# Softmax over rows of 1024: larger tiles, looped groups of four rows, and sixteen partitions of the first load sent ahead

## Chip, cores, metric

One core of a Trainium2 chip. The metric is device time in microseconds of one execution; executions of one kernel agree within 0.35% here. A packet below is one contiguous piece that one of the sixteen DMA engines moves; a wave is sixteen packets, one on each engine.

## The reference

```python
x = np.random.randn(32, 512, 1024).astype(np.float32)      # temperature 0.5
scaled = x / temperature
shifted = scaled - np.max(scaled, axis=-1, keepdims=True)
exp_x = np.exp(shifted)
return exp_x / np.sum(exp_x, axis=-1, keepdims=True)
```

16,384 rows of 4 KB are read once and written once, 134.22 MB in all. Laid over 128 partitions that is 128 rows per partition.

## The kernel before

A ring of six slots in SBUF, eight rows per partition in each. SyncE issues the loads, GpSimd the stores, VectorE takes the maxima and scales, ScalarE takes the exponentials with their sums.

```python
SLOTS, ROWS = 6, 8
GROUPS = [4, 2, 2]
# ... cut: sizes, tiles, semaphores
def dram(t, i):
    return t[P*ROWS*i : P*ROWS*(i+1), :].rearrange("(p k) d -> p k d", p=P, k=ROWS)

for i in range(tiles):                       # SyncE: loads
    if i >= SLOTS:
        nc.sync.wait_ge(stored[i % SLOTS], 16 * (i // SLOTS))
    nc.sync.dma_start(out=slot(i), in_=dram(xf, i)).then_inc(loaded[i % SLOTS], 16)
# ... cut: TensorE passes the loads on to VectorE in order
nc.gpsimd.wait_ge(loaded[2], 16)             # GpSimd: stores, from the third load on
for i in range(tiles - 1):
    nc.gpsimd.wait_ge(scaled, len(groups) * (i + 1))
    nc.gpsimd.dma_start(out=dram(of, i), in_=slot(i)).then_inc(stored[i % SLOTS], 16)

with nc.vector.Fori(0, tiles) as t:          # VectorE: groups written out
    take(nc.vector, ready)
    for a, k in groups:                      # maximum, then bias = -scale * maximum
        ...
    for a, k in groups:                      # wait for the sums, reciprocal, scale the rows
        ...
# ... cut: ScalarE, one activation per row; the last tile is stored by SyncE
```

Of the kernel before, what the change touches and what calls it, by code (L numbers as in the profile page):

```python
# [1 line left out]

# [4 lines left out]



SLOTS, ROWS = 6, 8  # L10

GROUPS = [4, 2, 2]


@with_exitstack
def kernel(
    ctx: ExitStack,
    tc: tile.TileContext,
    x: bass.AP,
    temperature: bass.AP,  # L20
    out: bass.AP,
):
    nc = tc.nc
    f32 = mybir.dt.float32
    scale = 1.0 / float(temperature)
    extreme = mybir.AluOpType.max if scale > 0 else mybir.AluOpType.min

    P = 128
    xf = x.flatten_outer_dims()
    of = out.flatten_outer_dims()  # L30
    n, d = xf.shape
    tiles = n // (P * ROWS)
    assert tiles * P * ROWS == n and sum(GROUPS) == ROWS
    groups = [(sum(GROUPS[:g]), k) for g, k in enumerate(GROUPS)]
    of_group = dict(groups)

    pool = ctx.enter_context(tc.tile_pool(name="data", bufs=1))
    ring = pool.tile([P, SLOTS * ROWS, d], f32, name="ring")
    top = pool.tile([P, ROWS], f32, name="top")
    bias = pool.tile([P, ROWS], f32, name="bias")  # L40
    sums = pool.tile([P, ROWS], f32, name="sums")
    recip = pool.tile([P, ROWS], f32, name="recip")
    warm = pool.tile([P, 1], f32, name="warm")



    loaded = [tc.alloc_semaphore(f"loaded{s}") for s in range(SLOTS)]
    stored = [tc.alloc_semaphore(f"stored{s}") for s in range(SLOTS)]
    ready, topped, biased, summed, inverted, scaled, finished = (
        tc.alloc_semaphore(name)  # L50
        for name in ("ready", "topped", "biased", "summed", "inverted", "scaled", "finished")
    )

    def dram(t, i):
        return t[P * ROWS * i : P * ROWS * (i + 1), :].rearrange("(p k) d -> p k d", p=P, k=ROWS)

    def slot(i):
        s = i % SLOTS
        return ring[:, ROWS * s : ROWS * (s + 1), :]

    def take(engine, sem, count=1):

        engine.wait_ge(sem, count).then_inc(sem, -count)  # L63

    with tc.tile_critical(no_gpsimd_drain=True):  # L65

        for i in range(tiles):
            if i >= SLOTS:
                nc.sync.wait_ge(stored[i % SLOTS], 16 * (i // SLOTS))
            nc.sync.dma_start(out=slot(i), in_=dram(xf, i)).then_inc(loaded[i % SLOTS], 16)  # L70
        for i in range(tiles):
            nc.tensor.wait_ge(loaded[i % SLOTS], 16 * (i // SLOTS + 1)).then_inc(ready, 1)


        nc.gpsimd.wait_ge(loaded[2], 16)
        for i in range(tiles - 1):
            nc.gpsimd.wait_ge(scaled, len(groups) * (i + 1))
            nc.gpsimd.dma_start(out=dram(of, i), in_=slot(i)).then_inc(stored[i % SLOTS], 16)  # L78

        with nc.vector.Fori(0, tiles) as t:  # L80
            first = t % SLOTS * ROWS
            take(nc.vector, ready)
            for a, k in groups:
                nc.vector.tensor_reduce(  # L84
                    out=top[:, a : a + k],
                    in_=ring[:, bass.ds(first + a, k), :],
                    axis=mybir.AxisListType.X,
                    op=extreme,
                ).then_inc(topped, 1)
                take(nc.vector, topped)  # L90
                nc.vector.tensor_scalar_mul(  # L91
                    bias[:, a : a + k], in0=top[:, a : a + k], scalar1=-scale
                ).then_inc(biased, k)
            for a, k in groups:
                take(nc.vector, summed, k)
                nc.vector.reciprocal(  # L96
                    recip[:, a : a + k], sums[:, a : a + k]
                ).then_inc(inverted, 1)
                take(nc.vector, inverted)
                for b in range(a, a + k):  # L100
                    row = ring[:, bass.ds(first + b, 1), :]
                    ins = nc.vector.tensor_scalar_mul(row, in0=row, scalar1=recip[:, b : b + 1])  # L102
                ins.then_inc(scaled, 1)


        nc.scalar.activation(  # L106
            warm, nc.const_aps.tensor(0.0, (P, 1)), mybir.ActivationFunctionType.Exp
        )
        with nc.scalar.Fori(0, tiles) as t:
            first = t % SLOTS * ROWS  # L110
            for b in range(ROWS):
                row = ring[:, bass.ds(first + b, 1), :]
                if b in of_group:
                    take(nc.scalar, biased, of_group[b])
                nc.scalar.activation(  # L115
                    row,
                    row,
                    mybir.ActivationFunctionType.Exp,
                    bias=bias[:, b : b + 1],
                    scale=scale,  # L120
                    accum_out=sums[:, b : b + 1],
                ).then_inc(summed, 1)


        i = tiles - 1
        nc.sync.wait_ge(scaled, len(groups) * tiles)
        nc.sync.dma_start(out=dram(of, i), in_=slot(i)).then_inc(finished, 16)
        for i in range(tiles - SLOTS, tiles - 1):
            nc.sync.wait_ge(stored[i % SLOTS], 16 * (i // SLOTS + 1))
    with tc.tile_critical(no_gpsimd_drain=True):  # L130
        nc.sync.wait_ge(finished, 16, synchronizes=[nc.sync.lower_ap(slot(tiles - 1))])


# [1 line left out]
_INS = ['x', 'temperature']  # L135
_OUTS = [((32, 512, 1024), 'float32')]

_NUMBERS = {'temperature': 0.5}


# [26 lines left out]
```

## Time and profile before

| what | value |
|---|---|
| median time, span of the profiled run | 318.5 us, 316.4 us |
| data moved, plateau rate | 134.22 MB, 434 GB/s |
| VectorE, ScalarE busy | 77%, 47% |
| data packets per DMA engine | 256 of 32 KB, 1.213 us each |
| first data packet starts, last one ends | 1.96 us, 314.6 us |

The kernel is a stream through sixteen DMA engines that are occupied from the second microsecond until 314.6 us.

### The profile page before, as it was taken

How to read it: one execution, taken by the hardware profiler on the slowest of the kernel's cores; microseconds unless marked ns; L12 is line 12 of the kernel's file. 1: busy time of each engine (PE TensorE's matmuls, PEld its weight loads, DVE VectorE, ACT ScalarE, POOL GpSimd, SP SyncE). 2: the span in 40 equal slices, each digit the busy share in tenths (PEclk: the TensorE clock that was granted, in tenths of full speed). 3: DMA queues.
4: the chain of work that ended last, by engine and by line, in shares of the span. 5: the costliest groups of instructions: out<-in, count | busy, mean ns of one | idle time of the engine just before them, and what ended most of it. 6: DMA issues, size and time to landing. Idle time of an engine off the chain costs nothing. (4 is left out here: it accounts for less than half of the span.)

```text
span 316.4 us, 1208 instructions
## 1 busy us (share of the span) xinstructions
DVE 244.4 (77%) x272; ACT 148.1 (47%) x258; POOL 8.3 (3%) x19
## 2 busy tenths in 40 slices
DVE  0299999999999999996959959598695977959600
ACT  1065555556464747380834709156090651907400
POOL 0000000000000000000000000000000000000000
DMA  8999999999999999999999999999999999999995
GB/s 319 410 456 406 398 447 414 456 406 456 423 447 418 439 435 431 439 423 443 418 443 418 452 414 456 423 439 427 435 443 418 447 418 443 418 452 406 456 423 253
DMA packets 4608, 134.22 MB, mean 424 GB/s; under 512 B 512, under 2 KB 512, under 8 KB 512
## 3 DMA queue, kind: packets, MB, share of 16 engines
q1 hardware_dynamic: 2448, 71.30, 52.7%
q0 software_dynamic: 2160, 62.92, 46.1%
HBM read 67.11 MB, written 67.11 MB: 424 GB/s over the span
## 5 line engine op out<-in xcount | busy, mean ns | idle before, releaser
L115 ACT ACTIVATE ring<-ring,bias x128 | 145.1, 1135 | 147.1 <-ACTq L63 147.1
L84 DVE TENSOR_REDUCE top<-ring 128x2 f32 (+1 forms) x48 | 143.8, 2996 | 39.4 <-DVEq L63 39.4
L102 DVE TENSOR_SCALAR ring<-ring,recip x128 | 89.1, 749 | 7.2 <-DVEq L63 1.8
L115 ACT ACTIVATION_READ_ACCUMULATOR ring<-ring,bias 128x1 f32 x128 | 24.0, 187 | 0.0
L78 POOL DMA_DIRECT2D out_dram<-ring x15 | 8.1, 542 | 271.1 <-DVE ring L102 238.5
L91 DVE TENSOR_SCALAR bias<-top 128x2 f32<-128x2 f32 (+1 forms) x48 | 8.2, 170 | 7.2
L96 DVE RECIPROCAL recip<-sums 128x2 f32<-128x2 f32 (+1 forms) x48 | 7.9, 164 | 0.0
L106 ACT ACT_TABLE_LOAD x1 | 1.3, 1283 | 0.9 <-SPq L65 0.9
L106 ACT ACTIVATE warm<-const-float32-0.0 128x1 f32<-128x1 f32 x1 | 0.2, 203 | 0.0
L148 POOL MEMSET const-float32-0.0<- 128x1 f32 x1 | 0.1, 99 | 0.2 <-issue 0.2
L148 POOL MEMSET const-bfloat16-1.0<- 128x1 bf16 x1 | 0.1, 102 | 0.0
L148 POOL MEMSET const-float32-1.0<- 128x1 f32 x1 | 0.1, 99 | 0.0
L148 POOL MEMSET const-uint8-127<- 128x1 uint8 x1 | 0.1, 99 | 0.0
## 6 DMA issues: line engine op xcount, KB each, us to landing
ring<-in_x_dram SPq DMA_DIRECT2D x16, 4096.0 KB, 49.4
out_dram<-ring POOLq DMA_DIRECT2D x15, 4096.0 KB, 44.0
out_dram<-ring SPq DMA_DIRECT2D x1, 4096.0 KB, 16.8
```

The source lines that it names most:

```text
L78: nc.gpsimd.dma_start(out=dram(of, i), in_=slot(i)).then_inc(stored[i % SLOTS], 16)
L84: nc.vector.tensor_reduce(out=top[:, a : a + k], in_=ring[:, bass.ds(first + a, k), :], axis=mybir.AxisListType.X, op=extreme,).then_inc(t ...
L91: nc.vector.tensor_scalar_mul(bias[:, a : a + k], in0=top[:, a : a + k], scalar1=-scale).then_inc(biased, k)
L96: nc.vector.reciprocal(recip[:, a : a + k], sums[:, a : a + k]).then_inc(inverted, 1)
L102: ins = nc.vector.tensor_scalar_mul(row, in0=row, scalar1=recip[:, b : b + 1])
L106: nc.scalar.activation(warm, nc.const_aps.tensor(0.0, (P, 1)), mybir.ActivationFunctionType.Exp)
L115: nc.scalar.activation(row, row, mybir.ActivationFunctionType.Exp, bias=bias[:, b : b + 1], scale=scale, accum_out=sums[:, b : b + 1],).th ...
L148: nc = _bacc.Bacc("TRN2", target_bir_lowering=False, num_devices=1)
```

## The change

The intent: fewer and larger transfers (tiles of twelve rows in four slots, the same ring bytes), shorter code (loops over groups in place of groups written out), and an earlier start: sixteen partitions, one for each DMA engine, are sent ahead of the rest of the first load.

```diff
-SLOTS, ROWS = 6, 8
-GROUPS = [4, 2, 2]
+TILES = [12] * 10 + [8]
+SLOTS = 4
+GROUP = 4
+AHEAD = 16
...
+            if i == 0:
+                nc.sync.dma_start(
+                    out=slot(0)[:AHEAD], in_=dram(xf, 0)[:AHEAD]
+                ).then_inc(opened, 16)
+                nc.sync.dma_start(
+                    out=slot(0)[AHEAD:], in_=dram(xf, 0)[AHEAD:]
+                ).then_inc(loaded[0], 16)
+            else:
+                nc.sync.dma_start(out=slot(i), in_=dram(xf, i)).then_inc(loaded[i % SLOTS], 16)
+        nc.tensor.wait_ge(opened, 16)
...
-            for a, k in groups:
+            with loop_groups(nc.vector, t) as g:
+                group = bass.ds(g * GROUP, GROUP)
                 # maximum and bias of one group, at register offsets
...
-            for a, k in groups:
+            with loop_groups(nc.vector, t) as g:
                 # reciprocal and scaling of one group
...                                        (ScalarE: the same loop, one semaphore count per group)
```

## The prediction

> **What bounds the kernel now.** I read the page first, then its DMA part, the windows, the GpSimd timeline and the packet records of the trace.

> ```profile
> span 316.4 us, 1208 instructions
> DVE 244.4 (77%) x272; ACT 148.1 (47%) x258; POOL 8.3 (3%) x19
> ...
> DMA  8999999999999999999999999999999999999995
> GB/s 319 410 456 406 398 447 414 456 406 456 423 447 418 439 435 431 439 423 443 418 443 418 452 414 456 423 439 427 435 443 418 447 418 443 418 452 406 456 423 253
> DMA packets 4608, 134.22 MB, mean 424 GB/s; under 512 B 512, under 2 KB 512, under 8 KB 512
> ...
> out_dram<-ring SPq DMA_DIRECT2D x1, 4096.0 KB, 16.8
> ```

> The reader is to see that the row of DMA digits is full from the second slice to the last but one, while no compute engine passes 77%. The kernel reads 67.11 MB and writes as much, and that is all its time is. Of the 4608 packets, 512 are the 4-byte semaphore writes of 32 transfers (16 each) and 4096 carry data, 256 per DMA engine, each 32 KB: one partition's eight rows.

> ```profile
> 0.00:5.00 5.00, 0.00 (x0) 1.49 (x2) 0.20 (x4) 1.00 0.62 210
> 5.00:10.00 5.00, 0.00 (x0) 0.00 (x0) 0.00 (x0) 1.00 1.05 452
> ...
> 100.00:200.00 100.00, 84.86 (x99) 54.27 (x96) 2.67 (x5) 1.00 1.00 434
> 200.00:280.00 80.00, 62.61 (x70) 36.65 (x64) 2.67 (x5) 1.00 1.00 434
> ...
> 310.00:317.00 7.00, 0.00 (x0) 0.00 (x0) 0.00 (x0) 1.00 0.40 173
> ```

> The last two numbers of each line are the DMA share and GB/s. The rate is 434 in the long middle, where loads and stores share the engines (short stretches jump about, as whole packets are counted in them). So 434 is this kernel's plateau, and 134.22 MB at 434 is 309.3 us. What is above it, 316.4 - 309.3 = 7.1 us, is all that any change to the schedule can win (2.2%). The packet records split it: the first data packet starts at 1.96 us, the sixteen engines begin within 0.8 us of each other, and their first packets take 1.4 to 2.5 us where later ones take 1.213 (about 0.7 us per engine lost). When the first store begins, around 35 to 38 us, some 29 packets are stretched, 0.9 us per engine. The engines end between 313.2 and 314.6, and the last completion is seen at 315.06 (298.21 + 16.8). Then 1.3 us to the end. The run is 1.8 us longer than the span (318.14 against 316.4); I carry that.

> ```profile
> 46.35 0.53 POOL L78 DMA_DIRECT2D out_dram<-ring  x1 [12.62 <-DVE ring L102]
> 62.45 0.53 POOL L78 DMA_DIRECT2D out_dram<-ring  x1 [15.57 <-DVE ring L102]
> ...
> 240.37 0.53 POOL L78 DMA_DIRECT2D out_dram<-ring  x1 [18.82 <-DVE ring L102]
> 259.74 0.53 POOL L78 DMA_DIRECT2D out_dram<-ring  x1 [18.84 <-DVE ring L102]
> 279.10 0.53 POOL L78 DMA_DIRECT2D out_dram<-ring  x1 [18.83 <-DVE ring L102]
> ```

> Two regimes: early stores come every 16.1 us, the pace of VectorE on a full ring; late ones every 19.36 us, the time of 8.39 MB at 433 GB/s, sixteen packets of 1.21 us on each engine. Two transfers' semaphore writes are inside that period and add nothing visible. GpSimd's idle time is put down to VectorE, but the pace is the DMA's.

> [...]

> **The change part by part.** Ring bytes are unchanged (48 rows per partition). One row of all partitions is 0.524 MB, 1.209 us at the plateau.

> 1. Larger packets. Ten tiles of 48 KB packets and one of 32 KB: per engine 2 x (10 x 8 + 8) = 176 packets, not 256. [...]
> 2. Fewer transfers: 22 + 1 (the split load) against 32, nine semaphore writes fewer on each engine at 9 ns: 0.1 us.
> 3. Sixteen partitions ahead. The first issue takes 0.38 us and packets begin 0.63 us after it, four of the engines 0.6 us after the others. With one descriptor per engine I estimate 0.2 to 0.4 us earlier: 0.3 us. The next issue follows after some 0.4 us and its descriptors are there before the first 48 KB packet (1.81 us) is done.
> 4. VectorE. A four-row group costs 4.70 us start to start for maximum and bias (13.71 to 18.41 us), a two-row group 2.58; reciprocal and scaling 2.98 and 1.64. Their sum for eight rows is 16.12, the early pace. Groups of four alone: 7.68 per four rows, 23.0 for twelve, 1.92 us per row against 2.015. [...] The DMA needs 24 x 1.209 = 29.0 us for the load and store of such a tile. [...] ScalarE needs 12 x 1.135 = 13.6 us, and its sums are ready before VectorE ends the maxima.
> 5. Does the coarser ring starve the DMA? By hand, both queues sharing equally when both have work: the third load lands at 2.7 + 36 x 1.21 + 0.6 = 46.8 us, the first store moves data from about 51 (before, too, its first packet at 37.3 came 4.2 us after its issue at 33.05). [...] The store queue starts stores 0 to 3 at 51, 75, 101 and 130 us: always after they are computed. The load queue is briefly empty around 71 to 78 us, between the fourth load and the first free slot, but stores flow then. Later loads are back to back, 29.0 us each. The last load (eight rows) is in at 273; VectorE is free at 278, and the last eight rows are done 17 to 19 us later, at 295 to 297. By then stores 8 and 9 would last until 302.6. So 5 us of queued stores cover the last tile's compute; before, the same cover was also 5 us (the last store issued at 298.2, the older stores alone would have lasted to 303.6). No gap.

> Sum: 0.4 + 0.1 + 0.3 = 0.8 us less, 317.8 us.

> **The rivals.** (a) [...] Against it: nothing in the trace; only that a start trimmed this finely would hardly have been left with so plain a loss[...]. I give it three in ten.
> (b) VectorE becomes the pace: if a loop turn costs 1 us[...], a tile takes 29 us, the cover of stores at the end is gone, and the last store starts 3 to 6 us late: 321 to 324 us. Against it: VectorE is 77% busy, and scalings of four rows (2.74 us) can hide the next turn's bookkeeping. One in twenty.
> (c) The start is worth more: the stretched first packets and the stretch at the first store come later or smaller, and the engines end closer together. All of it is 0.7 + 0.9 + about 1 us; winning half would give 316.5 us. One in six.

> **Range and chances.** The most that can be won is 2.2% and the parts I can size win 0.25%, so faster by over 2% is 2%. Slower by over 2% means more than 6.4 us lost, which only the harder half of (a) gives, with a little of (b): 14%. The rest, 84%, is within 2%. I put the point at 318.0, a little above the sum for the sake of (a), and the range at 316.3 to 324.5, skewed upwards for the same reason.

> **What would show it.** Right: 2816 data packets (3184 with the semaphore writes), a first slice a little above 319 GB/s, 434 in the middle, stores every 29.0 us, and the last store landing within a microsecond of 315 less 0.8. Wrong by (a): a first slice far below 319 GB/s, the first sixteen packets taking several times 1.8 us, engines ending microseconds apart. Wrong by (b): VectorE over 90% busy, DMA digits under 9 in the last fifth, and the last store issued after the previous one has landed.

The sum is 0.8 us less: 0.4 us for larger packets, 0.1 us for fewer semaphore writes (a 4-byte write takes 9 ns in the trace before) and 0.3 us for the earlier start, an estimate from the issue and start times beside it. The times of VectorE in step 5, from 278 us on, are an estimate that contains the cost of the loop turns. Rival (a) is that the sixteen partitions, and the 112 after them, load at a lower rate than all 128 together.

## The result

333.22 us median (332.77 to 333.88, six runs) against 318.48 us (318.01 to 318.76, six runs): ratio 1.0465, 95% interval 1.0451 to 1.0479. It is slower by 14.7 us and outside the predicted range.

From the page of the changed kernel:

```profile
span 331.4 us, 1879 instructions
DVE 237.5 (72%) x224; ACT 149.9 (45%) x258; POOL 5.7 (2%) x14
...
DMA  9898999999999999999999999999999999999996
GB/s 142 208 273 225 421 427 457 403 463 398 463 421 433 427 427 445 409 451 415 451 403 463 427 427 445 421 445 409 457 433 421 451 437 401 445 451 398 463 378 265
DMA packets 3184, 134.22 MB, mean 405 GB/s; under 512 B 368, under 2 KB 368, under 8 KB 368
```

The reader is to see the first four slices (0 to 33 us). The DMA digits say 9, 8, 9, 8: the engines are occupied. The GB/s below them say 142, 208, 273, 225, a third to two thirds of the plateau. From the fifth slice on the kernel runs as before. The packets number 3184, as predicted; what changed is how long the first ones took. The windows of the changed kernel (last two columns: DMA share, GB/s):

```profile
0.00:10.00 10.00, 0.00 (x0) 1.49 (x2) 0.20 (x4) 1.00 1.04 157
10.00:20.00 10.00, 0.00 (x0) 0.00 (x0) 0.00 (x0) 1.00 0.88 231
20.00:30.00 10.00, 0.00 (x0) 0.00 (x0) 0.00 (x0) 1.00 1.02 241
...
100.00:200.00 100.00, 85.02 (x83) 51.62 (x91) 2.13 (x4) 1.00 1.00 431
```

In the first 30 us, 6.3 MB arrive. At 434 GB/s from 2 us on it would have been 12.2 MB, and the missing 5.9 MB are 13.6 us of the plateau. The packet records agree. A 48 KB packet takes 1.815 us in the middle; the first sixteen, which began between 1.98 and 2.94 us, took 6.06 us on average, the next seven waves (the other 112 partitions) 2.6 to 4.35 us, the first wave of the second load 2.5 us, and from there on 1.82. Summed, the packets that began in the first 35 us took 15.6 us per engine more than their size calls for, against 0.7 us in the kernel before. Of the 15.6 us, 4.2 lie on the sixteen partitions sent ahead, 10.7 on the 112 behind them and 0.7 on the next wave: most of the loss is on the larger part. After 35 us it is 1.2 us here and 0.8 us before. The first packet did not begin earlier either: 1.98 us, where it was 1.96.

### The profile page after: what moved, and what is told of

It is laid out like the page before. It is cut to its first block, busy times and chain, and to the rows that moved or that the text cites. A ratio compares the mean times of both kernels' runs of the same rounds, so it can differ in the third digit from the quotient of the medians.

```text
span 331.4 us, 1879 instructions
## 1 busy us (share of the span) xinstructions
DVE 237.5 (72%) x224; ACT 149.9 (45%) x258; POOL 5.7 (2%) x14
## 2 busy tenths in 40 slices
DMA packets 3184, 134.22 MB, mean 405 GB/s; under 512 B 368, under 2 KB 368, under 8 KB 368
## 3 DMA queue, kind: packets, MB, share of 16 engines
HBM read 67.11 MB, written 67.11 MB: 405 GB/s over the span
## 5 line engine op out<-in xcount | busy, mean ns | idle before, releaser
L109 DVE TENSOR_REDUCE top<-ring x32 | 141.4, 4417 | 50.2 <-DVEq L70 34.9
L126 DVE TENSOR_SCALAR ring<-ring,recip x128 | 87.7, 749 | 13.2 <-DVEq L70 13.2
L142 ACT ACTIVATION_READ_ACCUMULATOR ring<-ring,bias x128 | 23.9, 187 | 0.0
L122 DVE RECIPROCAL recip<-sums x32 | 5.5, 173 | 8.0 <-DVEq L70 8.0
L116 DVE TENSOR_SCALAR bias<-top x32 | 5.5, 170 | 7.4 <-DVEq L70 7.4
L102 POOL DMA_DIRECT2D out_dram<-ring x10 | 5.5, 546 | 292.3 <-DVE ring L126 229.2
## 6 DMA issues: line engine op xcount, KB each, us to landing
ring<-in_x_dram SPq DMA_DIRECT2D x1, 4096.0 KB, 30.6
out_dram<-ring SPq DMA_DIRECT2D x1, 4096.0 KB, 13.7
```

The costliest lines, as they stand in the source:

```text
L109: nc.vector.tensor_reduce(out=top[:, group], in_=ring[:, bass.ds(first + g * GROUP, GROUP), :], axis=mybir.AxisListType.X, op=extreme,).th ...
L116: nc.vector.tensor_scalar_mul(bias[:, group], in0=top[:, group], scalar1=-scale).then_inc(biased, 1)
L122: nc.vector.reciprocal(recip[:, group], sums[:, group]).then_inc(inverted, 1)
L126: ins = nc.vector.tensor_scalar_mul(row, in0=row, scalar1=recip[:, bass.ds(g * GROUP + b, 1)])
L142: ins = nc.scalar.activation(row, row, mybir.ActivationFunctionType.Exp, bias=bias[:, column], scale=scale, accum_out=sums[:, column],)
```

## The experiments

My theory at this point was rival (a) of the prediction: the partitions that a load spans set its rate, and both the sixteen ahead and the 112 after them load at a lower rate than all 128. In the expectations below, its name and the mechanism that I gave for it, which no run shows, are cut; what follows a mark in the texts of e1 to e6 is what this theory expects. Its factors of two (e4, e6) and four (e5) were assumptions then; the measured ones stand below each text. Rival 1: the twelve-row tiles or the loops cost the time. Rival 2: any small, odd or additional first transfer costs it.

### e1_no_ahead: the split undone alone

```diff
-                (the two transfers of the first load)
+                nc.sync.dma_start(out=slot(0), in_=dram(xf, 0)).then_inc(loaded[0], 16)
-        nc.tensor.wait_ge(opened, 16)
```

> The changed kernel with the first load in one piece again. [...] the first packets take under 2.5 us, 434 GB/s from the second slice on, and the time is 317.8 us, between 317 and 319, against 333.2 for the changed kernel. Rival 1 (twelve-row tiles in four slots, or the looped groups, cost the time): it stays near 330 or above.

Measured: 319.45 us (five runs), ratio to before 1.0031 (1.0017 to 1.0045). The changed kernel's ratio is 1.0465, so the split alone costs 0.0434 x 318.5 = 13.8 us. Rival 1 is out as the main cause. The time stays 1.6 us above the 317.8 that I expected, just outside my 317 to 319; the runs e8 and e9 are about that.

```profile
0.00:10.00 10.00, 0.00 (x0) 1.49 (x2) 0.20 (x4) 1.00 0.85 329
10.00:20.00 10.00, 0.66 (x1) 0.00 (x0) 0.00 (x0) 1.00 1.04 452
20.00:30.00 10.00, 8.52 (x4) 4.64 (x8) 0.00 (x0) 1.00 0.98 423
```

The same windows as above: the DMA share is much the same, the rate 1.8 to 2.1 times as high.

### e2_before_ahead: the split alone, on the kernel before

```diff
+            if i == 0:
+                nc.sync.dma_start(out=slot(0)[:16], in_=dram(xf, 0)[:16]).then_inc(opened, 16)
+                nc.sync.dma_start(out=slot(0)[16:], in_=dram(xf, 0)[16:]).then_inc(loaded[0], 16)
... (cut: the other loads as they were; TensorE waits for `opened`)
```

> The kernel before with nothing but its first load split at partition 16, so packets of 32 KB. [...] the loss is proportional to the bytes of the first tile, eight rows in place of twelve, two thirds of the 15 us: 318.5 + 10 = 328.5 us, first packets near 4 us each where they took 1.9. Rival 1: 318.5, no change. Rival 2 (a fixed cost of a short or odd-sized transfer, not of its bytes): 318.5 + 15 = 333.

Measured: 326.68 us, ratio 1.0257, which is 8.2 us more. The first sixteen packets took 3.66 us on average. With two thirds of the bytes in the tile, the cost is 0.59 of 13.8 us: nearer to the 10 us of a cost that goes with the bytes than to the 15 us of a fixed cost of a transfer. It also shows the cost without the larger tiles and the loops.

### e3_ahead_rows: two transfers, each over all partitions

```diff
-                    out=slot(0)[:AHEAD], in_=dram(xf, 0)[:AHEAD]
+                    out=slot(0)[:, :GROUP], in_=dram(xf, 0)[:, :GROUP]
-                    out=slot(0)[AHEAD:], in_=dram(xf, 0)[AHEAD:]
+                    out=slot(0)[:, GROUP:], in_=dram(xf, 0)[:, GROUP:]
```

> The changed kernel with the first load split by rows: four rows of all 128 partitions go ahead, then eight rows. Two transfers as in the change, but each spans all partitions. [...] as without a split, 317.8 us, within 0.5 of the run without a split. Rival 2 (any small or second first transfer costs): above 325.

Measured: 319.36 us, ratio 1.0025, the same as without a split (1.0031). A second, smaller transfer in front costs nothing when it spans all the partitions. It gains nothing either: the first packet begins at 1.95 us. Its first window:

```profile
0.00:10.00 10.00, 0.00 (x0) 1.49 (x2) 0.20 (x4) 1.00 0.84 324
```

### e4_ahead_64: two equal halves

```diff
-AHEAD = 16
+AHEAD = 64
```

> The changed kernel with 64 partitions ahead in place of 16, so both parts are equal, even powers of two. [...] each packet takes 2 x 1.815 = 3.6 us and the twelve rows take 29 us in place of 14.5: 317.8 + 14.5 = 332.3 us. Rival 2 in its form 'the odd 112 or the tiny 16 are slow': near 318, as no part is odd or tiny.

Measured: 333.73 us, ratio 1.048, which is 14.3 us above the run without the split (14.5 expected). The eight first waves took 3.55 to 3.84 us per packet, 2.0 to 2.1 times 1.815; the next took 2.3 us, and from there on it was 1.82. No part is odd or tiny here, so with e3 rival 2 is out.

### e5_blocks and e6_strided: the same eight parts, in two places

Both load the first tile in eight transfers of sixteen partitions; the packets and the bytes are the same.

```diff
+                for part in range(8):                     # e5_blocks: neighbours
+                    nc.sync.dma_start(out=slot(0)[16*part : 16*part + 16], in_=(the same rows)) ...
+                for part in range(8):                     # e6_strided: every eighth partition
+                    nc.sync.dma_start(out=slot(0)[part:128:8], in_=(the same rows)) ...
... (cut: the two transfers that go; TensorE waits for all eight parts)
```

> The changed kernel with its first load in eight parts of sixteen neighbouring partitions. [...] all twelve rows at a quarter of the rate, 58 us in place of 14.5: 319.4 + 43.5 = 363 us, packets of 7.2 us. A theory of a cost per extra transfer (about 14 us for the first extra one): 319.4 + 7 x 14 = 417 us, or 333 if it is paid once.

> The same eight parts of sixteen partitions and the same packets, but each part takes every eighth partition[...]. [...] half the rate, 29 us in place of 14.5: 319.4 + 14.5 = 334 us, packets of 3.6 us. If the number of parts, of partitions in a part or the issue of them mattered and not their places: the same as the eight blocks of neighbours.

Measured: 359.01 us (ratio 1.1274) and 334.05 us (ratio 1.0495). The windows of e5_blocks, then of e6_strided:

```profile
10.00:20.00 10.00, 0.00 (x0) 0.00 (x0) 0.00 (x0) 1.00 0.69 79
20.00:30.00 10.00, 0.00 (x0) 0.00 (x0) 0.00 (x0) 1.00 1.39 157
30.00:40.00 10.00, 0.00 (x0) 0.00 (x0) 0.00 (x0) 1.00 0.69 79
```

```profile
0.00:10.00 10.00, 0.00 (x0) 1.49 (x2) 0.20 (x4) 1.00 0.92 192
10.00:20.00 10.00, 0.00 (x0) 0.00 (x0) 0.00 (x0) 1.00 0.96 202
20.00:30.00 10.00, 0.00 (x0) 0.00 (x0) 0.00 (x0) 1.00 1.15 236
```

A window counts a packet whole, so with packets of 6.9 us it swings between 79 and 157. The packet records give the rates. Sixteen packets, 0.786 MB, take 6.9 us on sixteen neighbours (114 GB/s), 3.82 us on every eighth partition (206 GB/s) and 1.815 us over all 128 (433 GB/s). That is close to a quarter, a half and the whole (0.26, 0.48 and 1). The number of parts and of partitions in them is equal in both kernels, so it is the places that count. The cost of e5_blocks over the run without a split is 39.6 us and not 43.5, mostly because sixteen packets moved at 114 GB/s and not at the quarter of 434, 108.5, that I had expected.

### e10_swap: SBUF partitions or HBM addresses?

e5 and e6 differ in the HBM addresses that a part reads as well. Here a part writes sixteen neighbours in SBUF and reads every eighth stretch of HBM; the first tile's rows come out permuted. Against e5_blocks:

```diff
-                        out=slot(0)[16*part : 16*part + 16], in_=dram(xf, 0)[16*part : 16*part + 16]
+                        out=slot(0)[16*part : 16*part + 16], in_=dram(xf, 0)[part:128:8]
```

> The eight parts of sixteen neighbouring partitions again, but each part reads every eighth of the 128 stretches of HBM that the strided parts read (the first tile's rows come out in another order, a wrong result on purpose). If the partitions of SBUF decide the rate: as the eight blocks, 359 us, packets of 6.9 us. If the addresses in HBM decide it: as the strided parts, 334 us, packets of 3.8 us.

Measured: 358.28 us (ratio 1.1249), packets of 6.85 us; the result is wrong. The SBUF side decides. One of its windows, as in e5_blocks:

```profile
10.00:20.00 10.00, 0.00 (x0) 0.00 (x0) 0.00 (x0) 1.00 0.69 79
```

### e7_mid: the split in the middle of the stream

```diff
+MID = 6
-            if i == 0:
+            if i == MID:          # the split of the load, and its wait, at the seventh tile
```

> The changed kernel with the split (16 and 112 partitions) moved from the first load to the seventh, in the middle, where stores flow on the other queue. If a slow packet holds its engine back and nothing fills the time: the same 13.8 us as at the start, 333 us. [...] half of it, 324 to 328 us. If stores hide it: 319.4 us.

Measured: 328.58 us, ratio 1.0315, which is 9.0 us above the run without the split. A third less is lost than at the start. The second case of the expectation, half of it, was for stores that take up part of the time; its wording is cut. That the stores on the other queue use this third is my reading; no run shows it apart. Between 140 and 150 us the rate still fell to 216 GB/s, so the estimate of half was a little too hopeful.

```profile
140.00:150.00 10.00, 7.94 (x16) 4.84 (x10) 0.00 (x0) 1.00 0.74 216
```

### e8_loops_only: loops, with tiles of eight rows

```diff
-TILES = [12] * 10 + [8]
-SLOTS = 4
+TILES = [8] * 16
+SLOTS = 6                       # on e1_no_ahead
```

> No split, tiles of eight rows in six slots as before, but the looped groups of four rows. The run without the split was 0.3% slower than the kernel before. If the tile size is what costs that (the last store starts later and meets stretched packets, coarser packets end further apart): 318.5 us, ratio 1.000. If the loops cost it: 319.4, ratio 1.003.

Measured: 327.70 us, ratio 1.0293 (1.0279 to 1.0307). Neither expectation held. The windows of the end:

```profile
300.00:305.00 5.00, 4.59 (x2) 4.63 (x8) 0.00 (x0) 1.00 1.07 459
305.00:310.00 5.00, 2.92 (x5) 4.63 (x8) 0.00 (x0) 1.00 0.00 0
310.00:315.00 5.00, 2.92 (x5) 0.00 (x0) 0.00 (x0) 1.00 0.24 105
315.00:320.00 5.00, 0.00 (x0) 0.00 (x0) 0.00 (x0) 1.00 0.98 419
```

The DMA engines stand still for some eight microseconds while VectorE and ScalarE finish the last tile: all earlier stores have landed by 306.5 us, and the last is issued at 313.59.

```profile
313.59 0.35 SPq L149 DMA_DIRECT2D out_dram<-ring  x1
```

The timeline of VectorE for one tile of this kernel (start, length, what, idle time before):

```profile
201.16 4.41 DVE L103 TENSOR_REDUCE top<-ring  x1
205.80 0.17 DVE L110 TENSOR_SCALAR bias<-top  x1 [0.24 <-DVEq L70]
206.49 4.42 DVE L103 TENSOR_REDUCE top<-ring  x1 [0.52 <-issue]
211.14 0.17 DVE L110 TENSOR_SCALAR bias<-top  x1 [0.23 <-DVEq L70]
211.71 0.18 DVE L116 RECIPROCAL recip<-sums  x1 [0.40 <-DVEq L70]
212.30 2.74 DVE L120 TENSOR_SCALAR ring<-ring,recip  x4 [0.41 <-DVEq L70]
216.63 0.18 DVE L116 RECIPROCAL recip<-sums  x1 [1.59 <-DVEq L70]
217.22 2.74 DVE L120 TENSOR_SCALAR ring<-ring,recip  x4 [0.41 <-DVEq L70]
219.87 4.41 DVE L103 TENSOR_REDUCE top<-ring  x1
```

A tile takes 219.87 - 201.16 = 18.71 us where the written-out groups took 16.12. The short idle times in brackets, 0.2 to 0.5 us, come with the loops; in the kernel before, VectorE waits at most 0.2 us within a tile. The 1.59 us before the second reciprocal is another thing: it cannot start until ScalarE has summed the group whose bias it got at 211.3. That wait has a second cause that I overlooked: the edit also changes the groups of a tile from 4, 2, 2 to 4, 4, so the last group has twice the rows to sum. No run has groups 4, 4 written out. An estimate from the traces: in e9_unrolled the second bias ends 9.4 us into a tile, four rows take ScalarE 4.5 us, the reciprocal and scaling of a group 3.0 us, and two hand-overs some 0.3 us each, together 17.5 us. Then about half of the 2.6 us would be the grouping and half the loops. 18.71 us is still under the 19.36 us that the DMA needs for a tile, and I had stopped at that comparison. But VectorE starts at 14.0 us, after the first load, and 14.0 + 16 x 18.71 = 313.4 us is when it ends. At the estimated 17.5 us it would be 294 us, so by this estimate the store is late only with the loops. Being faster than the DMA per tile is not enough; the gain over all the tiles must also cover the first load and the last store.

### e9_unrolled: twelve-row tiles, groups written out

```diff
-            with loop_groups(nc.vector, t) as g:        # on e1_no_ahead; ScalarE likewise
+            for a, k in [(0, 4), (4, 4), (8, 4)]:       # the last tile: (0, 4), (4, 2), (6, 2)
```

> No split, the twelve-row tiles in four slots, but the groups written out as before (4, 4, 4; the last tile 4, 2, 2). VectorE should take 23.0 us a tile (7.68 per four rows) where the loops take 26.2, and the last store be issued near 297 us in place of 302.4. If the loops are what made the run without the split 0.3% slower than before: 317.8 us, ratio 0.998. If the coarser tiles are: 319.4, ratio 1.003. Could be the fastest of all.

Measured: 318.39 us, ratio 0.9995 (0.9981 to 1.0009); the early stores come every 23.05 us and the last is issued at 297.01. Together with e8 this gives a square, as ratios to before:

| | groups written out | looped groups of four |
|---|---|---|
| tiles of eight rows | 1 (the kernel before, groups 4, 2, 2) | 1.0293 (groups 4, 4) |
| tiles of twelve rows | 0.9995 (4, 4, 4; last tile 4, 2, 2) | 1.0031 (4, 4, 4; last tile 4, 4) |

The larger tile alone changes nothing that can be measured. The looped groups cost 2.9% on eight-row tiles, there together with the coarser grouping, and 0.4% on twelve-row tiles, where only the last tile is grouped otherwise. The timeline of VectorE in e1_no_ahead shows why the twelve rows soften it:

```profile
193.31 0.18 DVE L116 RECIPROCAL recip<-sums  x1 [0.60 <-DVEq L70]
193.90 2.74 DVE L120 TENSOR_SCALAR ring<-ring,recip  x4 [0.41 <-DVEq L70]
196.56 0.17 DVE L116 RECIPROCAL recip<-sums  x1
197.14 2.74 DVE L120 TENSOR_SCALAR ring<-ring,recip  x4 [0.41 <-DVEq L70]
```

With a third group there is time for the sums: no 1.59 us before the second reciprocal. A tile takes 26.23 us, 2.19 us per row against 2.34 with eight rows. VectorE then ends early enough: the last store is issued at 302.43 us, and the older stores land only at 307.7. What the remaining 0.4% of e1_no_ahead is made of is not settled. Its trace has 0.55 us per engine of stretched packets where the last store begins, which e9_unrolled does not have, but why they stretch there no run shows.

No version beats the kernel before; e9_unrolled equals it.

## Why the prediction was wrong

**What bounds the kernel** was right. Between 100 and 200 us the rate is 431 to 435 GB/s in the kernels before and after and in e1, e8 and e9 (in e7_mid the split lies there). That at most 7 us were to be won no run contradicts.

**Step 3 of the parts, "sixteen partitions ahead", is the step that failed.** It expected 0.3 us earlier; the split costs 13.8 us (1.0465 against 1.0031). The start did not move at all (1.98 us against 1.96). The sixteen packets took up to 3.5 times as long as a packet of their size does later, those behind them up to 2.8 times. The cost that step 3 left out, fewer bytes per microsecond while not all partitions are spanned, was in the prediction as rival (a), and two of its signs came: the first slice at 142 GB/s, the first sixteen packets at 6.06 us. The third did not: the engines ended within 1.3 us of each other.

Two choices went wrong. I gave the rival three chances in ten although the argument against it was about how carefully the change looked to be made, not about the chip. Every transfer of the kernel before spans 128 partitions, so its trace could say nothing for or against the rival; a run like e2 could (8.2 us). And the upper end of the range, 324.5, left no room for the rival as it was measured, 333.2.

**Steps 1 and 2, larger and fewer packets:** 0.5 us were expected. The packet records show what step 1 could save: in an undisturbed load packets of 32 KB start 1.2094 us apart (kernel before) and packets of 48 KB 1.8117 us (e1_no_ahead), so 16 KB cost 0.6023 us and some 5 ns per packet are left that do not depend on size. For the 80 packets fewer on each engine that is an estimated 0.4 us. In the time it does not show. e9_unrolled, which has both steps and groups of four, has a ratio of 0.9995 with an interval of 0.9981 to 1.0009, that is 0.6 us less to 0.3 us more: not seen, not excluded. Its stretched packets add up to 2.2 us per engine against 1.6 in the kernel before, about as much as was to be saved.

**Step 4, VectorE's pace:** the arithmetic of written-out groups was exact (23.04 us a tile; e9_unrolled has 23.05). What I had put in for a loop turn no trace showed; by the traces it is (26.23 - 23.04) / 6 = 0.53 us on average, so the margin to the 29.0 us of the DMA is 2.8 us a tile and not the 6.0 of written-out groups. That a scaling of four rows can hide a turn held: in e1_no_ahead the reciprocal at 196.56 us follows the scaling (2.74 us) without idle time, while 0.73 and 0.72 us pass before the reduces at 182.35 and 187.89 us. In the changed kernel this stayed almost hidden, and rival (b) did not occur. In e8, with eight-row tiles, the store at the end did come too late: 9 us slower.

**Step 5, no gap in the DMA,** held for the changed kernel: the last store was issued at 316.39 us, and the older ones landed at 321.6, a cover of 5 us as predicted, although all of it came about 20 us later, 14 of them from the split. The sign "stores every 29.0 us" did not come: they were issued every 26.2 us to the end, at VectorE's pace, for VectorE waited for no load after the first.

**Rival (c)** did not occur: nothing was won at the start. In e1_no_ahead the stretch of the first packets and that at the first store are no smaller than before (0.9 and 1.0 us per engine against 0.7 and 0.8). In the changed kernel the stretch at the first store is absent, but 1.2 us lie elsewhere after the first 35 us, 0.5 of them at the last store. Over all the runs, the packets in flight are stretched when the first store begins, 0.8 us per engine with eight-row tiles (before, e8), 1.0 to 1.2 us with twelve-row tiles (e1, e3, e7, e9). In the six runs whose first load was cut by partitions (after, e2, e4, e5, e6, e10) this stretch is absent; why, no run shows.

## What to carry to other kernels

Let a load into SBUF span all 128 partitions, even the first small one; if a part is to go ahead, cut the load by rows. Here a cut by rows cost nothing (319.36 us against 319.45), and every cut by partitions cost 8 to 40 us; stores and cuts by columns were not tried. Read the DMA digits only with the GB/s beneath them: in the first 33 us of the changed kernel the digits were 8 and 9 while 142 to 273 GB/s flowed. When an engine runs beside a DMA-bound stream, check its whole length, first load and last store included, not its pace per tile alone; loops at register offsets and coarser groups used up that margin in e8 (18.71 us a tile against 16.12).
